# Gates added into the grid of experts by indirect DMAs of single values, in place of one-hot products

## The chip, the cores and the metric

The kernel runs on one core of one Trainium2 chip. The metric is device time in microseconds (us), as the median of several runs. The engines are named as in the profile: PE is TensorE, DVE is VectorE, ACT is ScalarE, POOL is GpSimd, and SP is the engine that issues most DMAs.

## The reference, cut to what matters

One layer of a streaming encoder works on 1024 prompt frames and 32 sample frames: a mixer (attention and a gated recurrence), then a layer of 16,384 one-neuron experts, and a last norm.

```python
n = RMSNorm(h)
h = h + (sigmoid(gA) * (a @ w_a) + sigmoid(gB) * (r @ w_b)) @ w_out     # a, r from n @ w_in
# experts: 8 heads, 128 x 128 experts, the best 16 of each head
sv, si = top_k(scores of the two halves of the keys, 16)
cv, ci = top_k(sv[0] + sv[1], 16);  e = si[0] * 128 + si[1];  gate = softmax(cv)
hid = gelu(einsum('thkd,td->thk', down[e], xn))
h = h + einsum('thk,thkd->td', gate * hid, up[e])
y = RMSNorm_final(h)
```

So each frame has 8 x 16 = 128 gates, each with the number of an expert. Inside a head the 16 numbers differ. The same expert may be named by two heads, and then its gates add up.

## The kernel before

**Frames.** Eight tiles of 128 prompt frames (0 to 7) and one tile of 32 sample frames ("S"). Tiles 0 to 4 (`DENSE`, 640 frames, `NV`) go through all 16,384 experts as large products. The other ones (`ROWS`) fetch the weights of their 128 experts per frame, one indirect DMA per expert column (`rows()`, L1044: 416 gathers of 128 rows of 8 KB).

**Stages.** `project` (L261 to L263 with tiles `gm`) multiplies the frames by w_in in two groups, tiles 0 to 4 and then the rest. Weights come in 512 KB units (L289). ACT rounds each to its upper part `wh` (L254) and POOL subtracts to get the lower part `wl` (L255), so each product is three matmuls. `natural` (L321) stores some of the projections through one single buffer `zn`. `stage_cd` makes the mixer's output and the scores of the experts for tiles 0 to 2, 3 and 4, and the rest. `topk(t)` finds the 16 best experts of each head on DVE, with a product on POOL for each head (L970, `oh`). `v_start` and `stage_v` run the 128 columns of experts for tiles 0 to 4: `hidden(e)` makes the hidden values of one column (weights split on ACT and POOL, `dh`, `dl`), `gated(e)` multiplies them by the gates of that column (L1214) and splits the result (`vwh`, `vwl`), and the loop over `jb` multiplies by the up weights (`uh`, `ul`) and adds to `acc`. Up to six columns of hidden values (`GE`) are made ahead of the gates.

**The grid of gates.** `scatter()` builds in DRAM the grid `W_d`, which holds the gate of each expert for each of the 640 frames, zero nearly everywhere. For each frame it makes a one-hot row of the expert's upper seven bits (`ohA`) and one of the lower seven (`ohB`, times the gate on POOL, L1139), and PE multiplies the two (L1090), which gives the frame's 128 x 128 gates. ACT copies four frames at a time to `stg` (L1091), and SP stores 16 frames in one DMA (L1095):

```python
equal(bm, 1)                                                   # DVE, L1126
G.tensor_tensor(out=bm, in0=bm, op=OP.mult, in1=...)           # POOL, L1139
PE.matmul(ps[:, u * 128:(u + 1) * 128], am[:, u], bm[:, u], start=True, stop=True)
```

`gated` loads the grid for `JB` = 8 columns of experts at a time (`gw`), and reads it with a step of eight values from frame to frame.

**Order of the work.** Five streams (large products, attention, routing, scatter, rows) are woven into one program by the time that each step is taken to cost (`SC`, `GC` and the numbers that are yielded). A scheduler then sets the order on each engine, and each engine works through its own in order. An engine that waits holds up all that stands behind it.

Of the kernel before, what the change touches and what calls it, by code (L numbers as in the profile page):

```python
# [7 lines left out]
F32 = mybir.dt.float32  # L8
# [37 lines left out]
RB, VR, VB, BB, OHB = 4, 3, 2, 4, 4  # L46
# engines that make the one-hot rows, in turn
AMS = "DA"
# [19 lines left out]
def step_kernel(ctx, tc, x_prompt, x_sample, cache_kT, cache_v, state, norm1, w_in, lam_params,  # L68
# [10 lines left out]
    wsp = ctx.enter_context(tc.tile_pool(name="wsp", bufs=1, space=PS))  # L79
# [25 lines left out]
    def ws_bank():  # L105
        return (P.get("wz") or wsp).tile([128, 512], F32, name="ws", tag="ws")
# [9 lines left out]
    iota_r = consts.tile([128, 128], F32, name="iota_r")  # L116
    G.iota(iota_r, pattern=[[1, 128]], base=0, channel_multiplier=0,
           allow_small_or_imprecise_dtypes=True)
    runs4 = consts.tile([128, 32], F32, name="runs4")
# [30 lines left out]
        # s - 16*(t//16) in 0..15 and s <= t  # L150
# [5 lines left out]
        # s - 32*(t//32) in 0..15, t in the second half of its 32  # L156
# [4 lines left out]
        # resets of the running sums at each block of 16  # L161
# [9 lines left out]
        # the weight of the second map  # L171
# [10 lines left out]
        # lower bounds of the gates, columns: heads  # L182
# [13 lines left out]
    # ---------------------------------------------------------------- scratch in DRAM  # L196
# [26 lines left out]
    def span(ts):  # L223
        """ runs of consecutive token columns: (first column here, first column in DRAM, width) """
# [32 lines left out]
    def mm3(out, pairs):  # L257
        """ sum of products of operands split into two parts each """
# [838 lines left out]
    def scatter():  # L1097
        """ the gates of some tiles, spread over the grid of all experts """
        late = None
# [353 lines left out]
```

## Time and profile before

| what | us |
|---|---|
| median of 3 runs | 3572.55 |
| lowest and highest run | 3564.31, 3581.58 |
| span of the profiled execution | 3583.5 |
| PE busy | 3257.4 (91%) |
| DVE busy | 3063.6 (85%) |
| POOL busy | 2074.9 (58%) |
| ACT busy | 1454.3 (41%) |

The profile shows one execution. The page gives its span and no run time of its own; the span lies 10.95 us (0.3%) above the median of the runs. A share of busy time is a mean over the span, and what a stage is limited by is read from the stretch of that stage. The three numbers of a row such as 936/1377/3914 are the least, the median and the greatest duration in ns.

### The profile page before, as it was taken

The page shows a single profiled execution, that of the slowest core. Times are in us where ns is not written, and L with a number is a line of the kernel's source. Part 1 is how long each engine was busy: PE and PEld are TensorE (multiplying, and loading weights), DVE is VectorE, ACT ScalarE, POOL GpSimd, SP SyncE. Part 2 cuts the span into 40 slices and gives each one's busy share as a digit, 9 for nine tenths or more (in the row PEclk, how much of TensorE's full clock was granted, in tenths as well). Part 3 has the DMA queues.
Part 4 walks back from the last instruction along what each step waited for, and adds up shares of the span by engine and source line. Part 5 has one row for each costly group of instructions (what it writes and reads, how often), then busy time and mean ns, then how long its engine had stood idle before and what let it go on. Part 6 is the DMA issues. An engine that isn't in the chain of part 4 may idle for free.

```text
span 3583.5 us, 59911 instructions
## 1 busy us (share of the span) xinstructions
PE 3257.4 (91%) x21639; PEld 3128.0 (87%) x21639; DVE 3063.6 (85%) x6101; ACT 1454.3 (41%) x3508; POOL 2074.9 (58%) x1339
## 2 busy tenths in 40 slices
PE   7999899989998887868989988899999999999995
PEld 7989899867877886767889888899999999999994
DVE  3354468999787999999999999988989989989998
ACT  3544334445665544543333323333333333333332
POOL 2322125546444556666666577777767666776674
PEclk9999999999998998978999999999999999999997
DMA  4554364454465644478788777799888998998987
GB/s 164 166 158 149 107 215 158 152 151 152 148 217 183 206 130 150 152 249 298 258 289 296 275 271 290 266 341 351 316 315 335 337 343 296 346 338 333 336 325 265
DMA packets 357304, 880.58 MB, mean 246 GB/s; under 512 B 30960, under 2 KB 190192, under 8 KB 299664
## 3 DMA queue, kind: packets, MB, share of 16 engines
q1 hardware_dynamic: 297104, 440.52, 36.8%
q0 software_dynamic: 59904, 436.23, 33.0%
q8 instruction: 171, 2.80, 0.3%
q14 instruction: 125, 1.02, 0.1%
HBM read 784.47 MB, written 92.14 MB: 245 GB/s over the span
## 4 chain that ended last, share of the span: by engine, by line
PE 28%; DVE 19%; issue 2%; DMA 2%; POOL 2%; ACT 0%; POOLq 0%; ACTq 0%; DVEq 0%
PE gv L263 9%; PE gv L262 9%; PE gv L261 9%; DVE row L1047 5%; DVE xp L1031 5%; DVE vg L1214 2%; DVE acc L1279 2%; DMA ur<-in_p_up_dram 2%; DVE vwl L255 2%; POOL row L1044 1%; DVE oh L967 1%; POOL dl L255 1%; DVE ef L972 1%; POOL ul L255 0%; DVE si L902 0%
## 5 line engine op out<-in xcount | busy, mean ns | idle before, releaser
L1044 POOL DMA_INDIRECT row<-in_p_rows_dram,ei x384 | 559.8, 1458 | 340.2 <-DVE xp L1031 172.2
L255 POOL TENSOR_TENSOR wl<-wr,wh 128x1024 fp32r<-128x1024 f32 x160 | 397.3, 2494 | 532.2 <-ACT wh L254 483.0
L261 PE MATMUL gv<-vxh,dh 128*128 128x320 f32 x2048 | 646.5, 316 | 42.4 <-DVE acc L1279 23.6
L263 PE MATMUL gv<-vxh,dl 128*128 128x320 f32 x2048 | 644.8, 316 | 34.8 <-POOL dl L255 34.7
L261 PE MATMUL gv<-vwh,uh 128*128 128x320 f32 x2048 | 636.2, 311 | 14.1 <-ACT uh L254 8.3
L262 PE MATMUL gv<-vwl,uh 128*128 128x320 f32 x2048 | 636.8, 311 | 12.4 <-DVE vwl L255 12.3
L262 PE MATMUL gv<-vxl,dh 128*128 128x320 f32 x2048 | 642.3, 314 | 0.0
L263 PE MATMUL gv<-vwh,ul 128*128 128x320 f32 x2048 | 633.9, 310 | 1.1 <-POOL ul L255 1.0
L1047 DVE CUSTOM_DVE_ANT_0 row<-row,xg 128x1024 f32<-128x1024 f32 x416 | 627.0, 1507 | 3.1 <-DMA sc<-scs 2.3
L1031 DVE SCALAR_TENSOR_TENSOR xp<-row,hid,xp 128x1024 f32<-128x1024 f32 x412 | 527.8, 1281 | 78.2 <-ACT hid L1050 78.0
L1049 ACT ACTIVATE hid<-hid 128x1 f32<-128x1 f32 x416 | 84.0, 202 | 936.1 <-DVE hid L1047 926.3
L255 POOL TENSOR_TENSOR ul<-ur,uh 128x512 fp32r<-128x512 f32 x256 | 359.7, 1407 | 135.2 <-ACT uh L254 125.6
L261 PEld LDWEIGHTS gv<-vxh,dh 128*128 128x128 f32 x2048 | 393.5, 192 | 50.1 <-DVE acc L1279 27.3
L263 PEld LDWEIGHTS gv<-vxh,dl 128*128 128x128 f32 x2048 | 392.7, 192 | 43.1 <-POOL dl L255 42.0
L255 POOL TENSOR_TENSOR dl<-dr,dh 128x512 fp32r<-128x512 f32 x256 | 365.1, 1433 | 82.0 <-ACT dh L254 73.9
L261 PEld LDWEIGHTS gv<-vwh,uh 128*128 128x128 f32 x2048 | 386.7, 189 | 17.1 <-ACT uh L254 9.3
L262 PEld LDWEIGHTS gv<-vwl,uh 128*128 128x128 f32 x2048 | 386.9, 189 | 16.5 <-DVE vwl L255 16.5
L262 PEld LDWEIGHTS gv<-vxl,dh 128*128 128x128 f32 x2048 | 393.9, 192 | 0.0
L263 PEld LDWEIGHTS gv<-vwh,ul 128*128 128x128 f32 x2048 | 386.3, 189 | 2.7 <-POOL ul L255 2.5
L1139 POOL TENSOR_TENSOR ohB<-ohB,tr 128x512 f32<-128x512 f32 x160 | 195.0, 1224 | 264.3 <-DVE ohB L1126 201.5
L1214 DVE TENSOR_TENSOR vg<-vg,gw 128x320 f32<-128x320 f32 x248 | 253.4, 1022 | 27.7 <-ACT vg L1174 17.5
L261 PE MATMUL gm<-xh,wh 128*128 128x320 f32 (+1 forms) x768 | 254.0, 331 | 0.0
(328 smaller groups left out, 7490.5 us busy)
## 6 DMA issues: line engine op xcount, KB each, us to landing
dr<-in_p_downT_dram SPq DMA_DIRECT2D x256, 256.0 KB
ur<-in_p_up_dram SPq DMA_DIRECT2D x256, 256.0 KB
wr<-in_w_in_dram SPq DMA_DIRECT2D x88, 512.0 KB
W_d<-stg SPq DMA_DIRECT2D x40, 1024.0 KB
gw<-W_d SPq DMA_DIRECT2D x32, 1280.0 KB
wr<-in_p_wq_dram SPq DMA_DIRECT2D x48, 512.0 KB
wr<-in_w_out_dram SPq DMA_DIRECT2D x24, 512.0 KB
wr<-in_w_a_dram SPq DMA_DIRECT2D x12, 512.0 KB
```

Source lines behind the costliest of these rows:

```text
L255: (lo_engine or G).tensor_tensor(out=l, in0=src, in1=h.bitcast(F32), op=OP.subtract)
L261: PE.matmul(out, lh, rh, start=(i == 0), stop=False)
L262: PE.matmul(out, lh, rl, start=False, stop=False)
L263: PE.matmul(out, ll, rh, start=False, stop=(i == n - 1))
L967: V.tensor_tensor(out=oh[:T], in0=cf[:T, h].unsqueeze(2).to_broadcast([T, 16, NCAND]), in1=iota_c[:T].unsqueeze(1).to_broadcast([T, 16, NC ...
L1031: V.scalar_tensor_tensor(out=acc, in0=row[:, D:], scalar=hid[:, k:k + 1], in1=acc if k else first, op0=OP.mult, op1=OP.add)
L1044: G.indirect_dma_start(out=row, out_offset=None, in_=p_rows, in_offset=bass.IndirectOffsetOnAxis(ap=ei[:, k:k + 1], axis=0))
L1047: V.tensor_tensor_reduce(out=row[:, 0:D], in0=row[:, 0:D], in1=xt, scale=1.0, scalar=0.0, op0=OP.mult, op1=OP.add, accum_out=h)
L1049: A.activation(h, h, AF.Gelu)
L1139: G.tensor_tensor(out=bm, in0=bm, op=OP.mult, in1=tr[:, 2, xs].unsqueeze(2).to_broadcast([128, 4, 128]))
L1214: V.tensor_mul(gh, gh, G_[h][:, :, j])
L1279: V.tensor_add(acc[:, db, cs], acc[:, db, cs], ps[:, :CHUNK])
```

## The change

The one-hot rows, their products, `stg` and the PSUM banks for them (`ws`) go. The grid is laid out anew, as 16,384 experts by 640 frames. At the start a new stream, `fill()`, stores zeros over all of it, in 80 DMAs of 512 KB on SP. `scatter()` then works out the place of each gate (`at`, one operation on DVE for each tile), and issues for each tile, head and rank one indirect DMA on POOL, which adds 128 single values, one of each frame, to the grid in DRAM: 5 x 8 x 16 = 640 DMAs. The 16 DMAs of a head need not wait for each other. Each DMA of a head waits until all 16 of the head before it (of the same tile) have landed, and those of a tile's first head wait for the zeros. `gated` loads four columns of experts at a time after all adds have landed, and multiplies 640 frames in one operation with a step of one. The number of banks for the large products is raised with the banks that come free, and the cost of a scatter step in the weave is set to 1.4. Comments are dropped; the diff leaves that out.

```diff
-JB = 8
+JB = 4
...
-GX = (3, 6, 3)
+GM, GX = 4, (4, 8, 4)
...
-GC, SC = 1.65, 1.0
+GC, SC = 1.65, 1.4
+
+ZF, ZC = 1024, 4.5
...
+    place = consts.tile([128, len(DENSE)], F32, name="place")
+    G.iota(place, pattern=[[128, len(DENSE)]], base=0, channel_multiplier=1,
            allow_small_or_imprecise_dtypes=True)
+    zero = mc.tile([128, ZF], F32, name="zero")
+    V.memset(zero, 0.0)
...
-    W_d = dram([128 // JB, 128, NV, JB], "W_d")
-    SB = 16
+
+    W_d = dram([16384, NV], "W_d")
+    W_one = W_d.rearrange("e (t o) -> (e t) o", o=1)
+    SYNC = mybir.DependencyInfo(mybir.DependencyClass.Sync, mybir.DependencyReason.DATA)
+    FILLS, LAST = [], []
+
+    def fill():
+
+        Wz = W_d.rearrange("(p e) t -> p (e t)", p=128)
+        for c in range(0, 128 * NV, ZF):
+            FILLS.append(SP.dma_start(out=Wz[:, c:c + ZF], in_=zero).ins)
+            yield ZC
...
-            while t not in ROUTE or "sct" not in P:
+            while t not in ROUTE:
                 yield None
-            sct = P["sct"]
             gate, ei = ROUTE[t]
...
-                    equal(bm, 1)
-                    G.tensor_tensor(out=bm, in0=bm, op=OP.mult,
-                                    in1=tr[:, 2, xs].unsqueeze(2).to_broadcast([128, 4, 128]))
+            q = DENSE.index(t)
+            at = P["pk"].tile([128, 128], I32, name="at", tag="at", bufs=2)
+            V.tensor_scalar(at, ei, float(NV), place[:, q:q + 1], op0=OP.mult, op1=OP.add)
+
+            before = FILLS
+            for h in range(PH):
+                key = "add%s.%d" % (t, h)
+                now = []
+                for k in range(h * 16, h * 16 + 16):
+                    i = G.indirect_dma_start(
+                        out=W_one, out_offset=bass.IndirectOffsetOnAxis(ap=at[:, k:k + 1], axis=0),
+                        in_=gate[:, k:k + 1], in_offset=None, compute_op=OP.add).ins
+                    tc.declare_no_dep(i, group=key, reason="no place twice in a head")
+                    tc.add_to_no_dep_group(key, i)
+                    for x in before:
+                        tc.add_manual_dep(i, x.name, SYNC, reason="one head's adds after another's")
+                    now.append(i)
                     yield SC
...
+                before = now
+            LAST.extend(before)
             DONE.add(t)
...
                 if j == 0:
-                    for h in range(2):
-                        G_[h] = P["gw"].tile([128, n // 2, JB], F32, name="gw", tag="gw", bufs=2)
-                        SP.dma_start(out=G_[h], in_=W_d[b, :, h * (n // 2):(h + 1) * (n // 2), :])
+                    G_[0] = P["gw"].tile([128, JB, n], F32, name="gw", tag="gw", bufs=2)
+                    i = SP.dma_start(out=G_[0], in_=W_e[:, e:e + JB]).ins
+                    for x in LAST:
+                        tc.add_manual_dep(i, x.name, SYNC, reason="all gates")
                 g = VX[e]
-                for h in range(2):
-                    gh = g[:, h * (n // 2):(h + 1) * (n // 2)]
-                    V.tensor_mul(gh, gh, G_[h][:, :, j])
+                V.tensor_mul(g, g, G_[0][:, j])
...
-        with tc.tile_pool(name="gm", bufs=3, space=PS) as P["gm"]:
+        with tc.tile_pool(name="gm", bufs=GM, space=PS) as P["gm"]:
...
-        with bank_pool("gv", 3) as P["gv"]:
+        with bank_pool("gv", 6) as P["gv"]:
             yield from v_start()
...
-        streams += [["routing", routing(), 0.0], ["scatter", scatter(), 0.0], ["rows", rows(), 0.0]]
+        streams += [["routing", routing(), 0.0], ["fill", fill(), 0.0], ["scatter", scatter(), 0.0], ["rows", rows(), 0.0]]
```

The change moves instructions on several engines. Three places are shown as they stand in the two programs. In these rows `xN` says that the instruction stands N times in a row.

**SP, the first projections** (`wr` are weights on their way in, `xt` frames, `v_d` and `out_dram` the stores of `zn`, L1084 the new zeros). Before:

```order
L348 DMA xt<-in_x_prompt_dram 128x1024
L289 DMA wr<-in_w_in_dram 128x1024 x3
L321 DMA v_d<-zn 128x256
L324 DMA out_dram<-zn 128x256
L348 DMA xt<-in_x_prompt_dram 128x1024
```

and with the change, where the first two rows are the store of the first `zn` and the two below the 55 zeros that of the second:

```order
L321 DMA v_d<-zn 128x256
L324 DMA out_dram<-zn 128x256
L1084 DMA W_d<-zero 128x1024
L289 DMA wr<-in_w_in_dram 128x1024
L1084 DMA W_d<-zero 128x1024 x3
L348 DMA xt<-in_x_prompt_dram 128x1024
L1084 DMA W_d<-zero 128x1024 x55
L321 DMA v_d<-zn 128x256
L324 DMA out_dram<-zn 128x256
L1084 DMA W_d<-zero 128x1024 x4
```

All 80 zeros now stand ahead of the store of the third `zn`, 55 of them in one piece between the first and the second. The waits of the same stretch with the change show that SP's DMAs take eight semaphores in turn (DMAHW0 to DMAHW7), so each one waits for the one eight before it:

```order
L1084 DMA W_d<-zero 128x1024 [waits DMAHW4_49]
L289 DMA wr<-in_w_in_dram 128x1024 [waits DMAHW5_49,Pool_49]
L1084 DMA W_d<-zero 128x1024 [waits DMAHW6_49]
L1084 DMA W_d<-zero 128x1024 [waits DMAHW7_49]
L1084 DMA W_d<-zero 128x1024 [waits DMAHW0_49]
L348 DMA xt<-in_x_prompt_dram 128x1024 [waits DMAHW1_49,DVE_49]
```

**POOL, the second group's projections** (`wl` is the lower part of a unit of weights, `ohB` the one-hot rows times the gates). Before:

```order
L255 TENSOR_TENSOR wl<-wr,wh 128x1024 x2
L1139 TENSOR_TENSOR ohB<-ohB,tr 128x512 x9
L255 TENSOR_TENSOR wl<-wr,wh 128x1024
L1139 TENSOR_TENSOR ohB<-ohB,tr 128x512 x2
L255 TENSOR_TENSOR wl<-wr,wh 128x1024
```

and with the change (L1111 are the adds; 10485760x1 is the grid, by single values):

```order
L1111 DMA W_d<-gate,at 10485760x1 x2
L255 TENSOR_TENSOR wl<-wr,wh 128x1024
L1111 DMA W_d<-gate,at 10485760x1 x13
L255 TENSOR_TENSOR wl<-wr,wh 128x1024
L1111 DMA W_d<-gate,at 10485760x1 x21
L255 TENSOR_TENSOR wl<-wr,wh 128x1024
```

Where up to nine operations on one-hot rows stood between two units of weights, up to 21 indirect DMAs stand now. At the end of a head the waits are these; the first add of the next head waits for all eight semaphores of POOL's DMAs, and inside a head an add waits for the one eight before it:

```order
L1111 DMA W_d<-gate,at 10485760x1 [waits DMASW6_49]
L1111 DMA W_d<-gate,at 10485760x1 [waits DMASW7_49]
L255 TENSOR_TENSOR wl<-wr,wh 128x1024 [waits DMAHW7_49,Activation_49]
L969 TENSOR_TENSOR oh<-oh,E 128x800 [waits DVE_49,Pool_49]
L255 TENSOR_TENSOR wl<-wr,wh 128x1024 [waits DMAHW0_49,PE_49,Activation_49]
L1111 DMA W_d<-gate,at 10485760x1 [waits DMASW4_49,DMASW5_49,DMASW3_49,DMASW6_49,DMASW2_49,DMASW7_49,DMASW1_49,DMASW0_49]
```

**POOL, the start of `stage_v`** (`row` are the gathers, `dl` and `ul` the lower parts of the experts' weights). Before, the end of the scatter:

```order
L1139 TENSOR_TENSOR ohB<-ohB,tr 128x512
L1044 DMA row<-in_p_rows_dram,ei 128x2048
L255 TENSOR_TENSOR dl<-dr,dh 128x512
L1139 TENSOR_TENSOR ohB<-ohB,tr 128x512
L255 TENSOR_TENSOR dl<-dr,dh 128x512
L1044 DMA row<-in_p_rows_dram,ei 128x2048
```

and with the change, the end of the adds:

```order
L1043 DMA row<-in_p_rows_dram,ei 128x2048 x3
L1111 DMA W_d<-gate,at 10485760x1 x15
L1043 DMA row<-in_p_rows_dram,ei 128x2048
L1111 DMA W_d<-gate,at 10485760x1
L1043 DMA row<-in_p_rows_dram,ei 128x2048 x7
L255 TENSOR_TENSOR ul<-ur,uh 128x512
```

Before, the last product for the grid stood behind 3 `dl` and 11 gathers; now the last add stands behind 14 `dl`, 2 `ul` and 36 gathers. From the first add to the last, POOL's order holds the 640 adds, 70 `wl`, 40 `oh`, 36 gathers, 14 `dl` and 2 `ul`. Of the adds, 230 stand behind the last `wl`.

## Rows read from the trace of the kernel before

**Rows 1.** Busy time by stretch: PE, PEld, DVE, ACT, POOL with instructions; clock, DMA, GB/s
```profile
0.00:20.00 20.00, 0.00 (x0) 0.00 (x0) 13.87 (x36) 6.44 (x7) 10.46 (x13) 1.00 0.74 256
20.00:60.00 40.00, 34.97 (x256) 33.20 (x257) 20.94 (x78) 13.79 (x29) 0.02 (x1) 1.00 0.36 119
90.00:400.00 310.00, 302.36 (x2159) 284.65 (x2158) 141.82 (x404) 140.81 (x346) 82.78 (x34) 0.99 0.46 146
740.00:1610.00 870.00, 738.08 (x4852) 667.69 (x4851) 787.78 (x1941) 463.46 (x1104) 478.13 (x289) 0.92 0.55 174
1657.00:3545.00 1888.00, 1802.55 (x12020) 1780.02 (x12021) 1769.67 (x2679) 650.73 (x1687) 1314.14 (x915) 0.99 0.85 312
2500.00:3000.00 500.00, 495.78 (x3361) 492.38 (x3361) 458.52 (x585) 177.07 (x465) 343.00 (x245) 1.00 0.88 324
```

**Rows 2.** The same view, 740 to 1610 us, of tile ohA, then of tile ohB
```profile
740.00:1610.00 870.00, 189.29 (x1280) 175.82 (x1280) 70.33 (x80) 150.02 (x397) 0.92 0.55 174
...
740.00:1610.00 870.00, 189.29 (x1280) 175.82 (x1280) 153.97 (x160) 195.03 (x160) 0.92 0.55 174
```

**Rows 3.** By source line: first index work, products of the scatter, first and last up product
```profile
L1106 DVE TENSOR_SCALAR ij<-ei x5: 160/226/1397, 731.6 to 1437.9; 128x128 int32<-128x128 int32 x5
L1090 PE MATMUL ws<-ohB,ohA x1280: 270/275/583, 746.7 to 1603.5; 128*128 128x128 f32 x183
L261 PE MATMUL gv<-vwh,uh x2048: 302/309/636, 1657.0 to 3545.2; 128*128 128x320 f32 x187
```

**Rows 4.** POOL's gathers: by source line, of the page, two in time
```profile
L1044 POOL DMA_INDIRECT row<-in_p_rows_dram,ei x384: 936/1377/3914, 1464.4 to 3562.1; - x192
...
L1044 POOL DMA_INDIRECT row<-in_p_rows_dram,ei x384 | 559.8, 1458 | 340.2 <-DVE xp L1031 172.2
...
1465.82 3.86 POOL L1044 DMA_INDIRECT row<-in_p_rows_dram,ei  x1 [0.30 <-issue]
1469.99 0.94 POOL L1044 DMA_INDIRECT row<-in_p_rows_dram,ei  x1 [0.30 <-DVE si L902]
```

**Rows 5.** POOL's other work, by source line
```profile
L255 POOL TENSOR_TENSOR wl<-wr,wh x160: 2335/2400/4252, 10.2 to 1487.5; 128x1024 fp32r<-128x1024 f32 x160
L970 POOL TENSOR_TENSOR oh<-oh,E x72: 1722/1765/3201, 673.0 to 2293.3; 128x800 f32<-128x800 f32 x64, 32x800 f32<-32x800 f32 x8
L255 POOL TENSOR_TENSOR dl<-dr,dh x256: 1262/1302/3415, 1540.4 to 3484.4; 128x512 fp32r<-128x512 f32 x128
```

**Rows 6.** SP and ACT in time: a store of zn is issued, and the next zn written
```profile
195.15 0.33 SPq L321 DMA_DIRECT2D i_d<-zn  x1
...
198.36 0.38 ACT L319 ACTIVATE zn<-gm 128x256 f32<-128x256 f32 x1 [1.13 <-DMA i_d<-zn]
```

**Rows 7.** ACT in time: the first three zn of the kernel
```profile
28.50 0.39 ACT L319 ACTIVATE zn<-gm 128x256 f32<-128x256 f32 x1 [1.27 <-PE gm L263]
...
33.70 0.38 ACT L319 ACTIVATE zn<-gm 128x256 f32<-128x256 f32 x1
37.32 0.38 ACT L319 ACTIVATE zn<-gm 128x256 f32<-128x256 f32 x1 [3.23 <-DMA out_dram<-zn]
```

**Rows 8.** DVE, of the page: the two operations of a gather, gating; then a split
```profile
L1047 DVE CUSTOM_DVE_ANT_0 row<-row,xg 128x1024 f32<-128x1024 f32 x416 | 627.0, 1507 | 3.1 <-DMA sc<-scs 2.3
L1031 DVE SCALAR_TENSOR_TENSOR xp<-row,hid,xp 128x1024 f32<-128x1024 f32 x412 | 527.8, 1281 | 78.2 <-ACT hid L1050 78.0
...
L1214 DVE TENSOR_TENSOR vg<-vg,gw 128x320 f32<-128x320 f32 x248 | 253.4, 1022 | 27.7 <-ACT vg L1174 17.5
...
L255 DVE TENSOR_TENSOR vwl<-vg,vwh x124: 795/830/4243, 1640.9 to 3505.3; 128x640 fp32r<-128x640 f32 x124
```

**Rows 9.** DMA queues of the page: packets, MB, share of 16 engines over the span
```profile
q1 hardware_dynamic: 297104, 440.52, 36.8%
q0 software_dynamic: 59904, 436.23, 33.0%
```

**Rows 10.** Waits from 740 to 1640 us, the first: us, times, longest
```profile
POOL ohB L1139 <- DVE ohB L1126: 201.5, 86, 9.6
```

More of the change, by code (lines that the diff above doesn't have):

```diff
@@ L44 @@
 PRE = [2, 1]
-RB, VR, VB, BB, OHB = 4, 3, 2, 4, 4
-AMS = "DA"
+RB, VR, VB, BB = 4, 3, 2, 4
 CSH = 2
-GX = (3, 6, 3)
+GM, GX = 4, (4, 8, 4)
 GB, GE = 2, 6
-GC, SC = 1.65, 1.0
+GC, SC = 1.65, 1.4
+ZF, ZC = 1024, 4.5
 PACED = dict(rows=(1, 2), routing=(0, 1, 2))
@@ L103, in gm_bank @@
         return P[key].tile([128, 512], F32, name="gm", tag="gm")
-    def ws_bank():
-        return (P.get("wz") or wsp).tile([128, 512], F32, name="ws", tag="ws")
     def dram(shape, name, dtype=F32):
@@ L857, in scores @@
                                   keysT[:, c], start=True, stop=True)
-                    pool = P.get("scp") or P.get("oh", wk)
-                    sb = pool.tile([128, 256], F32, name="scs", tag="scs", bufs=SCS[rings])
+                    sb = P.get("scp", wk).tile([128, 256], F32, name="scs", tag="scs", bufs=SCS[rings])
                     A.activation(sb[:T], ps[:T, 0:256], AF.Copy, scale=rs[i][:T])
@@ L1066, in rows @@
                 for c in range(2):
-                    ps = ws_bank()
+                    ps = gv_bank()
                     PE.matmul(ps[:T], runs4, full[:, c * 512:(c + 1) * 512], start=True, stop=True)
@@ L1085, in routing @@
             yield from topk(t)
-    def grid(t, s0, q, stg, am, bm):
-        ps = ws_bank()
-        for u in range(4):
-            PE.matmul(ps[:, u * 128:(u + 1) * 128], am[:, u], bm[:, u], start=True, stop=True)
-        A.activation(stg[:, :, q:q + 4, :].rearrange("p b t j -> p t b j"),
-                     ps.rearrange("p (t b j) -> p t b j", t=4, j=JB), AF.Copy)
-        if q + 4 == SB:
-            o = 128 * DENSE.index(t) + s0
-            SP.dma_start(out=W_d[:, :, o:o + SB, :].rearrange("b i t j -> i b t j"), in_=stg)
@@ L1097, in scatter @@
     def scatter():
-        late = None
         for t in [x for ts in CDG for x in ts if x in DENSE]:
-            while t not in ROUTE or "sct" not in P:
+            while t not in ROUTE:
                 yield None
-            sct = P["sct"]
             gate, ei = ROUTE[t]
-            ij = sct.tile([128, 2, 128], I32, name="ij", tag="ohA", bufs=2)
-            V.tensor_scalar(ij[:, 0], ei, 7, None, op0=OP.arith_shift_right)
-            V.tensor_scalar(ij[:, 1], ei, 127, None, op0=OP.bitwise_and)
-            ijf = sct.tile([128, 2, 128], F32, name="ijf", tag="ohA", bufs=2)
-            V.tensor_copy(out=ijf, in_=ij)
-            ps = ws_bank()
-            for j, src in enumerate((ijf[:, 0], ijf[:, 1], gate)):
-                PE.transpose(ps[:, j * 128:(j + 1) * 128], src, ident)
-            tr = sct.tile([128, 4, 128], F32, name="tr", tag="tr", bufs=1)
-            A.activation(tr[:, 0:3], ps.rearrange("p (a t) -> p a t", a=4)[:, 0:3], AF.Copy)
-            A.activation(tr[:, 3], ps[:, 0:128], AF.Copy, scale=-1.0)
-            for s0 in range(0, 128, SB):
-                stg = sct.tile([128, 128 // JB, SB, JB], F32, name="stg", tag="stg", bufs=1)
-                for q in range(0, SB, 4):
-                    pool, bufs = (P["oh"], OHB) if "oh" in P else (sct, 2)
-                    am, bm = [pool.tile([128, 4, 128], F32, name=x, tag=x, bufs=bufs)
-                              for x in ("ohA", "ohB")]
-                    xs = slice(s0 + q, s0 + q + 4)
-                    def equal(out, row):
-                        V.tensor_tensor(out=out, in0=iota_r.unsqueeze(1).to_broadcast([128, 4, 128]),
-                                        in1=tr[:, row, xs].unsqueeze(2).to_broadcast([128, 4, 128]),
-                                        op=OP.is_equal)
-                    if AMS[(s0 + q) // 4 % len(AMS)] == "A":
-                        for u in range(4):
-                            c = s0 + q + u
-                            A.activation(am[:, u], iota_r, AF.Abs, bias=tr[:, 3, c:c + 1])
-                        A.activation(am, am, AF.Relu, bias=1.0, scale=-1.0)
-                    else:
-                        equal(am, 0)
-                    equal(bm, 1)
-                    G.tensor_tensor(out=bm, in0=bm, op=OP.mult,
-                                    in1=tr[:, 2, xs].unsqueeze(2).to_broadcast([128, 4, 128]))
-                    yield SC
-                    if late:
-                        grid(*late)
-                    late = (t, s0, q, stg, am, bm)
-                    yield SC
-            grid(*late)
-            late = None
@@ L1203, in stage_v @@
             G_ = {}
+            W_e = W_d.rearrange("(i e) t -> i e t", i=128)
             def gated(e):
@@ L1326, in gemm @@
             P.pop("scp")
-            open_pool("oh")
             yield from until("B1")
             rings("right")
-            est["wz"] = ExitStack()
-            P["wz"] = est["wz"].enter_context(tc.tile_pool(name="wz", bufs=2, space=PS, side="right"))
-            yield from stage_cd(CDG[2], 2)
+            with tc.tile_pool(name="gx", bufs=GX[2], space=PS) as P["gx"]:
+                yield from stage_cd(CDG[2], 2)
+            P.pop("gx")
             ring.close()
         if stop == "mixer":
-            for key in ("oh", "sct", "mc"):
-                est[key].close()
+            est["mc"].close()
             return
@@ L1340, in gemm @@
         open_pool("xgp", space=PS)
-        with bank_pool("gv", 3) as P["gv"]:
+        with bank_pool("gv", 6) as P["gv"]:
             yield from v_start()
-        while not all(t in DONE for t in DENSE):
-            yield None
-        for key in ("oh", "sct", "mc"):
-            est[key].close()
-        P.pop("wz")
-        est["wz"].close()
-        PHASE[0] = 1
-        with bank_pool("gv", 5) as P["gv"]:
+            while not all(t in DONE for t in DENSE):
+                yield None
+            est["mc"].close()
+            PHASE[0] = 1
             yield from stage_v()
```

4 lines of the change are left out of this document (removed).

## The prediction

> **What bounds the kernel now.** I read the view of busy time by stretch first [rows 1]. The reader should see three regimes. From 90 to 400 us PE is busy 302 of 310 us, so a delay in the first projections goes through to the end. From 740 to 1610 us, where the grid is built, DVE is the fullest engine with 788 of 870 us; PE has 738, POOL 478. From 1657 to 3545 us, the products with the up weights [rows 3], PE is busy 1803 of 1888 us beside a DVE with 1770. How fast PE can go there shows from 2500 to 3000 us: 3361 matmuls in 500 us, 148.8 ns each, where DVE is busy 459 of 500.
>
> Next come the instructions of the scatter by line and tile [rows 2, 3]. It begins at 731.6 us, when the first tile has its experts, and its last product starts at 1603.5 us. The up products, which need the gates, follow 54 us later. So the end of the scatter opens the last stage, and that stage is about 1890 us of PE work. The third view is the waits [rows 10]: POOL waited 201.5 us for DVE's one-hot rows. POOL had room there, but only some 390 us of it (870 less 478).
>
> **What goes.** From 740 to 1610 us PE loses 189 us, DVE 70 + 154 = 224, ACT 150 and more for `stg`, POOL 195 [rows 2]. In the last stage a column of gates is one operation on 640 frames instead of two on 320. Before, 248 of these took 253 us [rows 8]. An operation of the new size on DVE has a median of 0.83 us there [rows 8], so 128 of them take 106, and DVE loses 147 us.
>
> **What comes, one: the zeros.** The 80 stores are 41.9 MB. In the first 20 us the DMA engines moved 256 GB/s at a share of 0.74, which is 346 GB/s when all are busy [rows 1], so the zeros alone take 121 us. The order decides where. Eight of SP's DMAs can be under way, all 80 zeros stand ahead of the third store of `zn`, and `zn` is a single buffer. The first 60 us move 9.9 MB of other data (256 GB/s x 20 us + 119 x 40) [rows 1]; 8 MB of it, and the zeros, are through at about 50 MB / 346 GB/s = 144 us. Before, the third `zn` was written at 37.3 us [rows 7]. ACT, which also rounds the weights, stands behind that `zn`, and PE has a few products and then no free bank. So the first projections come 100 us later. The bounds are 0 (the engines have room for 42 MB later on, at a share of 0.46 from 90 to 400 us) and 121. I take **100**, since the order is fixed and the wait is in it.
>
> **What comes, two: the adds, on POOL.** No row shows an indirect DMA that adds. The nearest are the gathers, with 128 indices each as well: 0.94 us on POOL at least, 1.38 as a median, 1.46 as a mean, and 0.30 us between one and the next [rows 4]. So an add costs 1.24 us by the least, 1.68 by the median and 1.76 by the mean. I take 1.45, about the middle between the least and the median, as an estimate: 640 x 1.45 = **928 us**. What lies between the first and the last add in POOL's order is 70 x 2.40 + 40 x 1.77 + 36 x (1.38 + 0.15) + 16 x 1.30 = **315 us** [rows 4, 5].
>
> **What comes, three: the waits between heads.** 35 heads wait until the 16 adds of the head before have landed. From the issue of a store to the next writing of its buffer 3.2 us passed [rows 6]. At more than half of the heads a `wl` or an `oh` stands between, which hides 1.8 to 2.4 us of it. I take 1.8 each, **63 us**, between 0 and 35 x 3.2 = 112. By the Trainium skill (DMA: Bandwidth & Descriptors, section Anatomy of one DMA — SWDGE (gpsimd) path) a DMA of POOL has a fixed cost of about 2.0 us, most of it the receipt of the write. By that estimate the waits would come to some 20 us, 40 less; the measured 3.2 us decides here.
>
> **What POOL's lateness holds up.** Behind the adds on POOL stand the `wl`, for which PE waits, and the `oh`, for which DVE waits in the routing of the next tiles. From the first add to the last POOL has 928 + 315 + 63 = **1306 us** of work in one order, where before there were 872 us. DVE and PE have less to do there than before, so POOL sets the pace, and what PE, DVE and ACT lose in this stretch is worth nothing. When the last `wl` is done 230 adds are still to come. PE can make six columns of hidden values ahead, 288 matmuls (43 us), and then stands still until the last add.
>
> **The last stage.** 12,288 less 288 = 12,000 matmuls remain, 1785 us at 148.8 ns. Before, they took 1888. DVE loses 147 us by the gates, and 25 more gathers (36 instead of 11) lie ahead of the stage, at 1.51 + 1.28 us of DVE each [rows 8], 70 us. So DVE has 1770 - 217 = 1553 us, 86% of 1810. From 2500 to 3000 us DVE was at 92% and PE at 99%, so I take **1810 us** (1785 to 1888).
>
> **The sum**, against the profiled execution of 3583.5 us:
>
> | | us |
> |---|---|
> | scatter begins, as before [rows 3] | 732 |
> | zeros | 100 |
> | adds, with all of POOL's work among them | 1306 |
> | first grid load, gating, split | 10 |
> | up products | 1810 |
> | tail after the last of them (3583.5 - 3545.2) | 38 |
> | end | 3996 |
>
> The median of the runs lies 11 us under that span, so I forecast **3985 us**, 11.5% slower. The 10 us are an estimate: a landing of 3.2 us, the load's own few us and two or three operations of 0.8 us.
>
> **The rivals.**
>
> *POOL's price is far lower (faster).* A gather moves 1 MB and an add 512 bytes. If POOL's time went with the bytes, an add might take 0.5 us or less, and POOL would fit. The end is 3068 + 640 times the price, so the point is (3583.5 - 3068)/640 = 0.80 us per add; below it the kernel is faster, and at 0.5 us it ends at 3388 us. DVE and PE allow about the same, 3583.5 + 100 - 224 - 78 = 3381. Against it: the gathers' times run from 0.94 to 3.9 us at one and the same size [rows 4], so bytes do not set them. 0.80 us is under the least of 384, and there would have to be no gap.
>
> *The DMA engines set the pace (much slower).* An add of 4 bytes needs a read of the grid, a sum and a write. 128 values over 16 engines are 8 per engine. A packet of POOL's queue held an engine for 0.33 x 16 x 3583.5 / 59904 = 0.316 us on average, one of the other queue 0.071 [rows 9]. At 0.071 an add takes 0.57 us of its engines, hidden under POOL; at 0.316 it takes 2.5 us, since only eight adds may be under way, and the end is 3068 + 1600 = about 4670 us. The point from which this decides is 1.45 / 8 = 0.18 us per value. Small packets of 4 bytes are not told apart in the rows. The Trainium skill (DMA: Bandwidth & Descriptors, section Specifications) says that writes under 512 bytes are read, changed and written back, which speaks for this rival; no row here gives its price.
>
> *The zeros cost nothing.* If ACT and PE get through, 100 us go and the end is 3885; with the adds at their least also, 3750. That is still slower, and inside the range.
>
> **How the numbers follow.** The forecast has 0.76. POOL fits and the kernel is faster: 0.11. An add between 0.77 and 0.83 us, which ends within 0.5% of before: 0.03. The DMA engines set the pace: 0.10. Inside the forecast the ends are, by adds at 1.24 or 1.76 us (-134, +198), zeros (-100, +21), waits (-63, +49) and the last stage (-25, +78): 3663 to 4331 with all on one side. The range of 3700 to 4380 leaves out the two outer rivals and little more. A change of under 0.5% is what a measurement of this kernel cannot tell from none; with that, faster has 0.11, within 0.5% 0.03, slower 0.86.
>
> **What would show it.** Right: by line, the 640 adds have a median on POOL between 0.94 and 1.7 us and end near 2130 us; the largest wait of PE (or of ACT for it) before the last stage leads to POOL or to the adds; from about 1800 us PE is nearly idle until the first up product; DMA is full up to 140 us with PE idle for some 100 of them; afterwards 12,000 matmuls in about 1810 us. Wrong: a last add before 1700 us would mean a price under 0.8 us, and the first rival; adds on POOL with long waits for DMAs inside a head would be the second; a third `zn` at 40 us would strike the zeros from the sum.

## The result and the profile after

The change runs in 4633.38 us (median of 4 runs, 4625.37 to 4638.5) where the kernel before took 3571.32 in the same comparison. The ratio is 1.296, with a 95% interval of 1.2925 to 1.299. That is 29.6% slower; the forecast was 3985 us with a range of 3700 to 4380.

The busy times and queues of the page of the kernel after (share of the span, instructions; packets, MB, share of 16 engines):

```profile
span 4636.7 us, 56852 instructions
PE 3145.9 (68%) x20344; PEld 3019.6 (65%) x20344; DVE 2770.6 (60%) x5724; ACT 1254.8 (27%) x2938; POOL 2853.7 (62%) x1819
q0 software_dynamic: 152064, 436.60, 30.5%
q1 hardware_dynamic: 226064, 440.52, 27.6%
```

PE and DVE have less to do than before, 3146 and 2771 us in place of 3257 and 3064, in a span that is 1053 us longer. POOL alone has more, 2854 in place of 2075, and even POOL stands at 62%. So the time went into waiting, and the stretches tell where. Busy time by stretch of the kernel after (the columns of [rows 1]):

```profile
60.00:144.00 84.00, 17.40 (x113) 16.36 (x114) 2.67 (x4) 7.06 (x13) 2.89 (x2) 0.56 0.86 344
90.00:400.00 310.00, 266.39 (x1893) 253.64 (x1894) 101.54 (x282) 118.98 (x273) 77.12 (x32) 0.92 0.55 187
816.00:2365.00 1549.00, 654.13 (x3723) 579.32 (x3723) 624.13 (x1785) 276.98 (x614) 1326.23 (x802) 0.70 0.42 88
2500.00:3000.00 500.00, 451.37 (x2859) 440.38 (x2859) 497.05 (x910) 156.75 (x398) 338.49 (x229) 0.95 0.77 279
3200.00:3300.00 100.00, 0.00 (x0) 0.00 (x0) 78.44 (x98) 15.90 (x64) 46.48 (x33) 0.50 0.91 342
4100.00:4600.00 500.00, 500.00 (x3414) 500.00 (x3413) 153.00 (x218) 139.14 (x245) 187.91 (x141) 1.00 0.29 98
```

Three holes of PE are to be seen. From 60 to 144 us it makes 113 matmuls while the DMA engines move 344 GB/s: the zeros. From 816 to 2365 us it is busy 42% of the time beside a POOL with 1326 us of records in 1549: the adds. And from 3200 to 3300 us, in the middle of the last stage, it makes not one matmul, and DVE, at 78 of 100 us, is the fullest engine. The last row is PE at its pace: 3414 matmuls in 500 us, 146 ns each, with DVE at 31%. The granted clock is full there, and at the lower of its two levels, 0.50, where PE stands still.

By source line, the adds, the first and the last up product, and the four products with which the sample tile's sums are made (count, least/median/greatest ns, first and last start):

```profile
L1111 POOL DMA_INDIRECT W_d<-gate,at x640: 1541/1549/3279, 816.4 to 2363.5; - x160
L261 PE MATMUL gv<-vwh,uh x2048: 302/309/636, 2387.1 to 4615.4; 128*128 128x320 f32 x187
L1067 PE MATMUL gv<-fnb,runs x4: 881/1044/1057, 3468.3 to 3470.8; 128*32 128x512 f32 x4
```

The waits of the whole kernel after (us in total, times, longest; rows of PEld, which repeat those of PE, left out):

```profile
PE gv L1067 <- DVE fnb L1064: 365.3, 1, 365.3
...
PE gm L263 <- POOL wl L255: 230.4, 27, 29.9
...
PE gv L261 <- ACT vwh L254: 172.2, 1, 172.2
```

The third of these is the wait for the last add, by way of the grid load and the gating. The second are the units of weights that stand behind adds on POOL. The first is not in the prediction at all: one wait of 365 us for `fnb`, a copy of the sample tile's sums on DVE.

Against the kernel before [rows 3], the 1053 us come in like this: the first add starts 85 us later than the scatter began (816.4 to 731.6); from there to the first up product 1571 us pass in place of 925, which is 645 more; the up products take 2228 us in place of 1888, 340 more; and the tail is 17 us shorter. The sum is 1053.

The theory after this reading: POOL's own work for an add is dearer than was taken (A), and the hole at 3100 to 3467 us is a matter of the order of work and not of load. The rivals: it is the sum in the DMA that costs (B), or DVE, with 497 of 500 us before the hole, is simply too full (C).

### The profile page after: what moved, and what is told of

It reads as the page before. It is cut to its first block, busy times and chain, and to the rows that moved or that the text cites. A ratio compares the mean times of both kernels' runs of the same rounds, so it can differ in the third digit from the quotient of the medians.

```text
span 4636.7 us, 56852 instructions
## 1 busy us (share of the span) xinstructions
PE 3145.9 (68%) x20344; PEld 3019.6 (65%) x20344; DVE 2770.6 (60%) x5724; ACT 1254.8 (27%) x2938; POOL 2853.7 (62%) x1819
## 3 DMA queue, kind: packets, MB, share of 16 engines
q0 software_dynamic: 152064, 436.60, 30.5%
## 5 line engine op out<-in xcount | busy, mean ns | idle before, releaser
L1111 POOL DMA_INDIRECT W_d<-gate,at x640 | 1030.9, 1611 | 209.3 <-issue 175.6
L1043 POOL DMA_INDIRECT row<-in_p_rows_dram,ei x384 | 544.0, 1417 | 418.3 <-DVE xp L1030 293.0
L255 POOL TENSOR_TENSOR wl<-wr,wh 128x1024 fp32r<-128x1024 f32 x160 | 410.7, 2630 | 558.2 <-ACT wh L254 520.0
L1046 DVE CUSTOM_DVE_ANT_0 row<-row,xg 128x1024 f32<-128x1024 f32 x416 | 602.8, 1449 | 197.2 <-DMA row<-in_p_rows_dram,ei 187.7
L255 POOL TENSOR_TENSOR dl<-dr,dh 128x512 fp32r<-128x512 f32 x256 | 344.4, 1357 | 223.3 <-ACT dh L254 220.7
L1188 DVE TENSOR_TENSOR vg<-vg,gw 128x640 f32<-128x640 f32 x124 | 192.3, 1551 | 283.2 <-ACT vg L1148 283.1
L263 PE MATMUL gm<-act,wl 128*128 128x384 f32 (+2 forms) x576 | 194.6, 348 | 201.9 <-POOL wl L255 200.6
```

Source lines behind the costliest of these rows:

```text
L255: (lo_engine or G).tensor_tensor(out=l, in0=src, in1=h.bitcast(F32), op=OP.subtract)
L263: PE.matmul(out, ll, rh, start=False, stop=(i == n - 1))
L1043: G.indirect_dma_start(out=row, out_offset=None, in_=p_rows, in_offset=bass.IndirectOffsetOnAxis(ap=ei[:, k:k + 1], axis=0))
L1046: V.tensor_tensor_reduce(out=row[:, 0:D], in0=row[:, 0:D], in1=xt, scale=1.0, scalar=0.0, op0=OP.mult, op1=OP.add, accum_out=h)
L1111: i = G.indirect_dma_start(out=W_one, out_offset=bass.IndirectOffsetOnAxis(ap=at[:, k:k + 1], axis=0), in_=gate[:, k:k + 1], in_offset=Non ...
L1188: V.tensor_mul(g, g, G_[0][:, j])
```

## The experiments

Each but two is the changed kernel with the edit shown, and its time stands against 4633 us of the change; the two with one tile by adds are the kernel before with an edit. The kernel before, which ran beside them all, took 3573 to 3580 us. The kernel with both repairs ran four times and the two with one tile by adds five times each, the others once.

### Writes in place of adds

```diff
-    in_=gate[:, k:k + 1], in_offset=None, compute_op=OP.add).ins
+    in_=gate[:, k:k + 1], in_offset=None).ins
```

> Leaves out the sums: each indirect DMA writes its 128 values in place of adding them, so a gate whose expert two heads share is overwritten. Everything else as in the change. Theory A (POOL's own work for an indirect DMA of single values sets its price, the sum costs POOL nothing): median on POOL stays at 1.55 us, 1.86 us from one to the next, the last one still starts near 2364 us, the span stays within 20 us of 4637. Rival B (the sum is what makes POOL's 1.55 us): the median falls to the gathers' 0.94 to 1.0 us, 640 x 0.6 = some 380 us less, last one near 1980 us, span near 4250.

It took 4273.2 us. By source line, and of the page, this kernel's indirect DMAs:

```profile
L1111 POOL DMA_INDIRECT W_d<-gate,at x640: 953/958/2726, 814.3 to 2007.0; - x160
...
L1111 POOL DMA_INDIRECT W_d<-gate,at x640 | 669.7, 1046 | 206.7 <-issue 174.8
...
q0 software_dynamic: 80384, 436.60, 27.8%
```

Theory A fell, and B came close to its numbers. The same instruction, with the same 128 places and values, holds POOL 0.96 us when it writes and 1.55 us when it adds; the time between two is the same (175 us of "issue" in both). The last one starts 357 us earlier and the span is 365 us shorter, so nearly all of POOL's gain goes through to the end. The queue shows a second difference: a DMA that adds took (152064 - 59904) / 640 = 144 packets, one that writes (80384 - 59904) / 640 = 32.

The wait for `fnb` is still there, 361.6 us: it doesn't hang on the adds' price.

### The sample tile last

```diff
-ROWS = [5, 6, "S", 7]
+ROWS = [5, 6, 7, "S"]
```

> The sample tile's gathers come after those of tile 7; POOL's order up to the last add is unchanged (36 gathers among the adds), and in PE's order the four products for the sample tile's sums stand behind 3744 of the 6144 up products, where they stood behind 2160. Theory A (the 365 us that PE stands still there are an effect of its order alone, PE can make the up products at its own pace): last add near 2364 us as before, PE's wait for those products under 60 us, span near 4637 - 365 = 4270. Rival C (DVE, at 497 of 500 us from 2500 to 3000, is what bounds the stage, and the wait only shows it): PE keeps to some 5.5 matmuls per us until the gathers end and waits in small pieces for gates and sums; 165 us or less come back at first sight, span 4360 or more.

It took 4713.7 us, 80 more than the change. PE's wait, and busy time from 3000 to 3500 us:

```profile
PE gv L1067 <- DVE fnb L1064: 432.7, 1, 432.7
```

```profile
3000.00:3500.00 500.00, 495.62 (x3362) 492.42 (x3361) 456.44 (x545) 171.89 (x458) 340.68 (x246) 1.00 0.89 326
```

Theory A fell. Rival C's time came (4360 or more), but not its account, which was a slower PE with waits in small pieces: PE keeps its pace up to the sample tile's products (3362 matmuls in 500 us), so DVE doesn't bound the stage. The wait moved with the products, to 3576 to 4009 us, and grew. What the two programs have in common shows in DVE's order, counted between the gating and the sums of two columns: in the change 117 rows of gathers stand in one piece after the 49th gating, here 140 in one piece after the 82nd. Elsewhere it is 3 at most, apart from the 39 and 6 ahead of the first columns. 365.3 / 117 = 3.12 us and 432.7 / 140 = 3.09 us a row: PE waits for exactly that piece. In the kernel before, no piece is longer than 7. So the question became why no gating stands among these rows; the banks, tried in the fifth experiment, are the answer.

### The zeros spread out

```diff
             FILLS.append(SP.dma_start(out=Wz[:, c:c + ZF], in_=zero).ins)
+            last = [i for i in nc.cur_bb.bb.instructions if i.engine == PE.engine]
+            if last:
+                tc.add_manual_dep(FILLS[-1], last[-1].name, SYNC, ...)
-ZF, ZC = 1024, 4.5
+ZF, ZC = 1024, 7.0
```

> Each of the 80 stores of zeros waits for a PE instruction, so that they are spread over the first projections and the attention in SP's order; nothing else differs. Theory A (the zeros at the start delay all by what PE lost there, and POOL's adds carry it to the end): the third zn near 37 us, the first add near 732 to 740 us in place of 816, span 76 to 84 us shorter, near 4557. Rival D (the engines' 121 us are paid wherever they lie, or SP's waits for PE hold up the loads of weights behind them): first add after 780 us, span over 4600.

It took 4537.6 us, 96 less. First the kernel after, then this one: ACT in time, the first three `zn` (start, us, engine, line).

```profile
24.68 0.38 ACT L319 ACTIVATE zn<-gm 128x256 f32<-128x256 f32 x1 [1.63 <-PE gm L263]
...
44.87 0.38 ACT L319 ACTIVATE zn<-gm 128x256 f32<-128x256 f32 x1 [1.80 <-DMA out_dram<-zn]
...
122.32 0.38 ACT L319 ACTIVATE zn<-gm 128x256 f32<-128x256 f32 x1 [68.93 <-DMA out_dram<-zn]
```

```profile
26.31 0.38 ACT L319 ACTIVATE zn<-gm 128x256 f32<-128x256 f32 x1 [1.14 <-PE gm L263]
...
31.82 0.38 ACT L319 ACTIVATE zn<-gm 128x256 f32<-128x256 f32 x1
39.45 0.39 ACT L319 ACTIVATE zn<-gm 128x256 f32<-128x256 f32 x1
```

Theory A holds: the third `zn` goes from 122 us back to 39, near the 37 of the kernel before [rows 7], the first add from 816.4 to 742.4 us. The stretch of the adds stays what it was (1548 us from the first to the last), and the start of the stretch goes through to the end. The span is 101 us shorter, where 76 to 84 were expected: 74 come from the start, 8 more by the first up product, and 19 in the last stage, which no run explains.

The zeros now reach past the first adds. By source line, the adds and the zeros of this run:

```profile
L1114 POOL DMA_INDIRECT W_d<-gate,at x640: 1540/1548/2997, 742.4 to 2290.6; - x160
L1084 SPq DMA_DIRECT2D W_d<-zero x80: 319/327/904, 2.1 to 873.1; - x80
```

The last 8 of the 80 zeros are issued from 750.0 to 873.1 us, after the first adds. They cover a tenth of the grid, and a gate of tile 0 that was added there ahead of them is overwritten with zero. So this run leaves out some of the gates, and so do the two with both repairs below. What they show of the time stands; a true repair would need all zeros ahead of the first add.

### Half of the adds

```diff
-for k in range(h * 16, h * 16 + 16):
+for k in range(h * 16, h * 16 + 8):
```

> Leaves out the adds of ranks 8 to 15 of each head, 320 of 640. Theory A (POOL's order sets the pace of the whole stretch, at 1.86 us an add): last add 320 x 1.86 = 595 us earlier, near 1770 us, and the span about as much shorter, near 4040 if the wait of PE for the sample tile stays as it is. Rival E (with POOL relieved, routing on DVE and the weights set the end of the stretch): last add after 1850 us, and POOL with over 150 us of waits for DVE and ACT among the adds.

It took 3884.6 us, 749 less. By source line:

```profile
L1111 POOL DMA_INDIRECT W_d<-gate,at x320: 1540/1555/4855, 816.1 to 1803.0; - x160
```

The last add starts 560 us earlier, 1.75 us for each add left out (1.86 was expected): POOL's order does set the pace of the stretch, and rival E's sign, a last add after 1850 us, did not come. The span fell by 190 us more than that. With 320 fewer steps of the scatter the weave is another one, the piece of rows in DVE's order is 60 long, and PE's wait is 185.7 us, 180 less than in the change: 3.10 us a row for the third time.

### A bank of its own for the sample tile

The change took the banks `ws` away, and the sample tile's products, which had used them, now draw theirs from the same rotation `gv` as the hidden values and the up products (L1066).

```diff
-gb_bank, gv_bank = bank_of("gb"), bank_of("gv")
+gb_bank, gv_bank, ws_bank = bank_of("gb"), bank_of("gv"), bank_of("ws")
...
-                    ps = gv_bank()
+                    ps = ws_bank()
                     PE.matmul(ps[:T], runs4, full[:, c * 512:(c + 1) * 512], ...)
...
-        with bank_pool("gv", 6) as P["gv"]:
+        with bank_pool("gv", 5) as P["gv"], bank_pool("ws", 1) as P["ws"]:
```

> The four products of the sample tile's sums get a PSUM bank of their own (as before the change, where they used ws), and the up products take turns in five banks in place of six. Nothing is different on POOL up to the last add; in DVE's order 223 gathers' rows stand ahead of the gating of column 64, where 338 stood, and in PE's order the four products stand behind 3936 up products in place of 2160. Theory F (sharing one rotation of banks is what put 115 rows in one piece ahead of the next columns, and at 3.1 us each they are PE's 365 us): PE's wait for fnb under 40 us, last add still near 2364 us, up products in some 1860 us, span 4637 - 365 = 4272 (4230 to 4330). Rival C2 (the gathers end near 4010 to 4030 us whatever the order, in the change and with the sample tile last alike, so PE waits as long in other places): span 4450 or more.

It took 4279.6 us; 4272 was expected. By source line (up products, the sample tile's), the adds, and PE's waits from 2380 us on:

```profile
L261 PE MATMUL gv<-vwh,uh x2048: 302/309/634, 2390.1 to 4256.7; 128*128 128x320 f32 x187
...
L1067 PE MATMUL ws<-fnb,runs x4: 592/604/617, 3635.9 to 3641.2; 128*32 128x512 f32 x4
...
L1111 POOL DMA_INDIRECT W_d<-gate,at x640: 1540/1549/3277, 816.4 to 2365.5; - x160
```

```profile
PE gv L261 <- ACT vwh L254: 176.7, 1, 176.7
PE gv L262 <- DVE vwl L255: 20.3, 18, 2.7
...
PE ws L1067 <- DVE fnb L1064: 0.2, 1, 0.2
```

Theory F holds. Up to the last add the times are the same within 2 us, the wait of 365 us is 0.2 us, and the up products take 1866.6 us. The mechanism is told by the programs, and shown by the edit alone: banks of a rotation are handed out in the order in which the program is written, so the columns written after the sample tile's products wait for banks that are free only when those are done, and all rows up to the sample tile had to come first. In the kernel before these products had `ws`, and PE's wait for `fnb` was 0.3 us.

### Both repairs

The edits of the spread zeros and of the bank, in short:

```diff
+                tc.add_manual_dep(FILLS[-1], last[-1].name, SYNC, ...)
...
+        with bank_pool("gv", 5) as P["gv"], bank_pool("ws", 1) as P["ws"]:
```

> The own bank and the spread zeros together. If both act by themselves, as theories A for the zeros and F for the bank say, the savings add up: 4633 - 96 (as measured with the zeros alone) - 365 = 4172 us, 4130 to 4230. If F's rival holds, 4350 or more. In both cases slower than the kernel before, since the 640 adds with 1.86 us of POOL each are still ahead of the last stage.

It took 4175.1 us, 1.167 times the kernel before (1.1654 to 1.169). The two savings add up to within 3 us of the expectation. What is left over the kernel before, about 600 us, is for the most part POOL's order: the adds run from 742.1 to 2292.9 us, and the first up product starts at 2307.1 us, 650 later than before [rows 3]. Here too the last 8 zeros stand behind the first adds.

### One tile by adds, four by one-hot products

The kernel before, with tile 0's gates added into a grid of their own:

```diff
+    ADD = DENSE[0]
+    W_a = dram([128 // JB, 128, 128, JB], "W_a")
...
+    def adds():
+        ...
+                i = G.indirect_dma_start(
+                    out=W_one, out_offset=bass.IndirectOffsetOnAxis(ap=at[:, k:k + 1], axis=0),
+                    in_=gate[:, k:k + 1], in_offset=None, compute_op=OP.add).ins
...
-        for t in [x for ts in CDG for x in ts if x in DENSE]:
+        for t in [x for ts in CDG for x in ts if x in DENSE and x != ADD]:
```

> The kernel before, with the gates of tile 0 alone placed by 128 adds, in a grid of its own of 8 MB (zeros spread over the first projections), and tiles 1 to 4 by one-hot products as before. Tile 0 takes a fifth of the one-hot work with it: PE 38, DVE 45, ACT 30, POOL 39 us; POOL gains 128 x 1.86 = 238. Theory A (an add costs POOL 1.86 us and nothing else that is scarce, so adds are a gain as long as POOL has room, and from 740 to 1610 us it had 390 us): POOL fits, the end of the scatter and with it the last stage come up to 45 us earlier, 3530 to 3565 us. Rival H (POOL's order is what counts, not its sum: the units of weights behind runs of up to 16 adds come late for PE in the second group's projections): 3600 us or more.

It took 3659.4 us, 1.0227 times the kernel before (1.0212 to 1.0242). Theory A fell, and rival H's time came. Busy time from 740 to 1000 us, of the kernel before and then of this one:

```profile
740.00:1000.00 260.00, 233.62 (x1480) 201.46 (x1478) 223.63 (x471) 135.94 (x346) 133.99 (x80) 0.95 0.50 150
```

```profile
740.00:1000.00 260.00, 200.87 (x1135) 172.41 (x1135) 153.85 (x418) 82.42 (x194) 224.71 (x130) 0.87 0.49 110
```

POOL has 225 of 260 us where it had 134. DVE and PE are busy 70 and 33 us less, and nothing moves up into their room: the next tile's index work starts at 987.5 us, where it started at 941.9. The scatter ends at 1671.6 us in place of 1603.5, and the first up product is 70 us later, which is most of the loss. PE's waits for units of weights from 740 to 1700 us, before and then here:

```profile
PE gm L263 <- POOL wl L255: 1.9, 1, 1.9
```

```profile
PE gm L263 <- POOL wl L255: 26.5, 7, 9.9
PE gm L262 <- POOL wl L255: 17.2, 3, 8.6
```

So H's mechanism is there. It is not the whole loss: POOL's first `oh`, ahead of all adds, starts at 686.9 us in place of 673.0. These 14 us belong to something else, perhaps to the 8 MB of zeros; that was not tried.

### The same with tile 2

```diff
-    ADD = DENSE[0]
+    ADD = DENSE[2]
```

> As the hybrid with tile 0, but it is tile 2 whose gates are added. In the kernel before, tile 2 comes at 1115 us, and from 1200 to 1610 us DVE was 97% busy and POOL about 60%; tile 0's one-hot work lay at 740 to 940 us, where DVE was at 86% and the next tile came only at 942 us. Theory A2 (tile 0's hybrid lost because nothing could move up into the room that it left, while its adds made the units of weights late): here the 45 us of DVE go from the stretch that DVE sets, the scatter ends 20 to 45 us earlier than before, 3535 to 3565 us. Rival H2 (POOL's order: the one-hot rows of the other tiles and the units of weights stand behind runs of up to 18 adds, 33 us each, and DVE and PE wait for them, whichever tile it is): 3600 us or more.

It took 3701.4 us, 1.0328 times the kernel before (1.0301 to 1.0355). Rival H2 holds. Busy time from 1000 to 1200 us, of the kernel before and then of this one, the adds, and PE's longest wait from 1000 to 1300 us:

```profile
1000.00:1200.00 200.00, 178.97 (x1342) 158.88 (x1340) 172.66 (x422) 124.34 (x300) 105.03 (x62) 0.93 0.66 209
```

```profile
1000.00:1200.00 200.00, 126.79 (x769) 105.25 (x769) 90.34 (x215) 67.07 (x184) 169.94 (x104) 0.74 0.52 106
```

```profile
L1113 POOL DMA_INDIRECT W_a<-gate,ei x128: 1548/1564/4221, 917.5 to 1224.6; - x128
```

```profile
PE ws L1138 <- POOL ohB L1187: 63.5, 8, 21.4
```

While the adds run, DVE falls to 90 us in 200 and PE to 127; in the kernel before they had 173 and 179 there. PE waits up to 21.4 us at a time for one-hot rows that stand behind adds on POOL. So adds for a fifth of the frames already cost time, in a stretch where POOL had been busy only half of it. A2's own condition was not met: the adds came from 917 to 1225 us, ahead of most of the stretch from 1200 to 1610 us that it wanted to relieve, so what they would cost inside that stretch is open.

### Writes, with both repairs

The kernel with both repairs, and

```diff
-    in_=gate[:, k:k + 1], in_offset=None, compute_op=OP.add).ins
+    in_=gate[:, k:k + 1], in_offset=None).ins
```

> The own bank and the spread zeros, and plain writes in place of adds, which leaves out the sums of gates whose expert two heads share. If the three savings are independent: 4175 - 360 (the writes alone gave 4633 - 4273) = 3815 us, 3780 to 3850. If they overlap (POOL no longer sets the pace at 1.26 us a write), over 3870. Either way over the kernel before: the price at which this change would break even was put at 0.80 us.

It took 3830.6 us; 3815 was expected. The last write starts at 1953.2 us, 340 us earlier than the last add with both repairs (2292.9). The last 8 zeros stand behind the first writes here as well. So even a DMA of single values at 0.96 + 0.30 = 1.26 us leaves this kernel some 250 us slower than before. No version that was tried beats the kernel before.

## Why the prediction was right or wrong

The direction was right and the size was not: the kernel ended at 4636.7 us where the sum said 3996. Two steps failed: the price of an add, and the last stage. By the terms of the sum:

| term | predicted | measured | difference |
|---|---|---|---|
| first add starts (scatter begins, zeros) | 832 | 816.4 | -16 |
| from there to the end of the last add | 1306 | 1548.6 | +243 |
| first up product after it | 10 | 22.1 | +12 |
| up products | 1810 | 2228.3 | +418 |
| tail | 38 | 21.3 | -17 |
| end | 3996 | 4636.7 | +641 |

**The zeros: right.** 100 us were taken and the first add starts 85 us later. The third `zn` was written at 122 us behind the zeros on SP, by the mechanism told, and spreading them gave the time back.

**The adds on POOL: the mechanism was right, the price was mis-sized.** "I take 1.45, about the middle between the least and the median" of the gathers. An add measured 1.55 us and 0.30 to the next, 1.86 in a row; with all gaps it is (1030.9 + 209.3) / 640 = 1.94 us, above even the upper bound of 1.76. With the heads' waits in it that is 1240 us against 928 + 63, the whole of the 243. Writing alone would have cost 0.96 + 0.30 = 1.26, close to the gathers at their least (1.24): what was missed is the sum, 0.59 us of POOL for 128 values, which no row of the kernel before showed. The bounds were those of another instruction, and the cost of the part that it lacks was put at nothing.

**The waits between heads: over-sized.** 63 us were taken, from the 3.2 us of a store of `zn` [rows 6]. Of the waits for earlier adds, by the source line of the adds in the kernel after, there remained:

```profile
DMA W_d<-gate,at: 18.3, 11
```

The Trainium skill (DMA: Bandwidth & Descriptors, section Anatomy of one DMA — SWDGE (gpsimd) path) had led to an estimate of some 20 us, and the measured 18.3 us agrees with it in the sum. That is luck in part, for 35 waits had been counted. With the sample tile last, where the profile tells the landing of some of the same adds, these took from issue to landing (least/median/greatest, us)

```profile
DMA to landing us min/median/max: 2.8/3.0/7.7
```

so the 3.2 us of the row were about right. What was over-sized is how much of it shows: 11 waits of 1.7 us on average, where 35 of 1.8 were taken.

**POOL sets the pace: right.** Leaving out half of the adds brought the last one 1.75 us per add earlier, and from 816 to 2365 us POOL waited only some 25 us for other engines, so PE's and DVE's savings in the stretch were worth nothing, as told.

**The last stage: the step that failed most.** "From 2500 to 3000 us DVE was at 92% and PE at 99%, so I take 1810 us", from the sum of DVE's work in the stage (1553 us, 86%). With the sample tile's bank apart the stage takes 1867 us, inside the bounds of 1785 to 1888. The other 362 us are a wait that no sum of busy times shows: the sample tile's products and the up products share one rotation of banks, and 117 rows of gathers stand in one piece in DVE's order. The order of the changed kernel was there to be read, and these products stand in it behind 2160 up products where they had stood behind 4224; the prediction read the order on POOL and SP alone.

**DVE's gain by gating: over-sized, without effect.** 106 us were taken for 640 frames at once; the 124 operations on `vg` took 192 us. Sorted by what POOL does beside them, the trace of the kernel after tells the two cases apart. Of the 37 beside which POOL ran no operation on two tensors, none took more than 0.88 us. Of the 80 that began while POOL was at one, such as `dl`, 74 took 1.40 us or more, 1.70 in the median, and 55 ended 0.68 to 0.70 us after POOL's operation did. One such pair in time (start, us):

```profile
4101.05 1.29 POOL L255 TENSOR_TENSOR dl<-dr,dh 128x512 fp32r<-128x512 f32 x1 [0.47 <-ACT dh L254]
4101.32 1.70 DVE L1188 TENSOR_TENSOR vg<-vg,gw 128x640 f32<-128x640 f32 x1 [7.44 <-ACT vg L1148]
```

So the price of 0.83 us held only where POOL left DVE alone. No edit tried this. In the stretch after the gathers, where nearly all took 1.70, DVE is at 31% and the longer time cost nothing.

**The rivals.** POOL's price was far from 0.80 us. The DMA engines did not set the pace: from 1200 to 1700 us the queue shows, in the kernel after,

```profile
q0 software_dynamic: 31189, 0.12, 16.3%
```

which is 0.163 x 16 x 500 / 31189 = 0.042 us of an engine for a packet, below both 0.071 and 0.316, and some 6 us of 16 engines, 0.38 us, for an add. That rival's 4670 us lies near the result, but it is reached on another way. The zeros were not free.

## What to carry to other kernels

An instruction that the trace doesn't show is not priced by its nearest relative when an option, here a sum, is added to it: its bound above has to lie well over the relative's. When a change removes a small private resource such as a PSUM bank, ask who used it besides, which rotation that user joins now, and whether in the new order of an engine a long piece of other work stands ahead of what it waits for. And room on an engine, read as span less busy time, is not room in its order: moving one tile of five to 128 adds, with the zeros for them, cost the kernel 2 to 3%, in stretches where POOL had been idle for nearly half of the time. A stream that clears memory must be done before the first value is added to it: when the order of a program is loosened for speed, that has to be read from the new trace again.

## What was not expected of the hardware

An indirect DMA that adds holds POOL 1.55 us where one that writes the same 128 single values holds it 0.96 us, and it takes 144 packets in place of 32. What POOL does in the 0.59 us more is not shown. From 1200 to 1700 us the adds' packets took 16.3% of the DMA engines (the row above); the queue of the kernel that writes has in the same stretch

```profile
q0 software_dynamic: 8757, 0.16, 1.3%
```

The record of an add reaches into what follows. In the kernel after, POOL in time (start, us):

```profile
1704.47 1.56 POOL L1111 DMA_INDIRECT W_d<-gate,at  x1 [0.30 <-issue]
1705.48 2.34 POOL L969 TENSOR_TENSOR oh<-oh,E 128x800 f32<-128x800 f32 x1
1707.99 1.57 POOL L1111 DMA_INDIRECT W_d<-gate,at  x1 [0.16 <-issue]
1709.87 2.24 POOL L1111 DMA_INDIRECT W_d<-gate,at  x1 [0.31 <-issue]
```

The product `oh` starts 1.0 us after the add, and its record is 2.34 us long in place of 1.74 to 1.77. Between two adds 1.86 us pass. So the rows of two POOL operations can hold the same time twice where one follows an add: from 816 to 2365 us the records add up to 1387 us, and cover 1326. The pace of a run of adds is read from their starts.
